# The last phase of a streaming encoder layer: row stores and x loads on GpSimd's DMA queue

## The chip, the cores and the metric

The kernel runs on one core of a Trainium2 chip. The core has a matrix engine (TensorE, PE in the profile; its weight loads are PEld), VectorE (DVE), ScalarE (ACT), GpSimd (POOL) and SyncE (SP). Each engine executes its own instruction stream in order; an instruction that waits for a semaphore holds everything behind it on that engine. DMA transfers are started by an instruction on one of these streams and carried out by 16 DMA engines that all streams share. The metric is the device time of one execution in microseconds, the median of several runs.

## What is computed

One layer of a chunk-causal encoder with two token mixers, for 2048 rows of a new stream and for 8 running streams of 16 rows that have 512 rows of cached keys and values each. Cut to what matters for the last phase:

```python
def merge_branches(oa, ob, za, zb, ga, gb, subln_g, lam_init, w_branch_a, w_branch_b, w_out):
    oa = rms_norm(oa, subln_g) * (1.0 - lam_init)
    ya = (oa.reshape(b, s, WIDTH_A) * jax.nn.silu(za)) @ w_branch_a
    yb = (ob.reshape(b, s, WIDTH_B) * jax.nn.silu(zb)) @ w_branch_b
    return (jax.nn.sigmoid(ga) * ya + jax.nn.sigmoid(gb) * yb) @ w_out
...
xp = xp + gate * merge_branches(...)
...
y_prompt = rms_norm(xp, final_g)
y_sample = rms_norm(xs, final_g)
```

`oa` and `ob` are the outputs of a differential attention and of a stick-breaking attention, both computed earlier. D_MODEL is 1024, both branch widths are 512. The sample rows need their attention over the cache too, and that work has been left for the last phase, where it runs between the matmuls.

## The kernel before

The rows are cut into 17 tiles of 128: 16 of the prompt and one (number 16, `NT`) that holds all sample rows. Earlier phases project the inputs and compute the attention of the prompt rows; they leave attention outputs in `o_d`, the gate inputs z in `z_d` and the merge gates in `g_d`, all in HBM. The last phase, from L1460 on, is a software pipeline over the tiles in the order 0 to 14, 16, 15 (`tiles`, L1379). One pass of its loop (L1593) is called a slot here. Slot n contains, for different tiles at once:

- `inputs(tiles[n + 2])` (L1311): loads of o and z into the single buffers `hs[0:2]` (L1318, L1319) and of the gates (L1325); o times z on GpSimd (L1330); scaling on VectorE (L1338), sums of squares on ScalarE (L298), a power-of-two scale on VectorE (L243 and on), and a split into two half-precision parts (L318 on ScalarE, L323 on VectorE).
- `turned(tiles[n + 1])` (L1369): transposition of these halves on TensorE (L1308, copied out on ScalarE in L1309), or from `MOVED` = 12 on by a DMA transpose (L1373).
- `branches(tiles[n])` (L1492): four groups of 12 matmuls (L1501), whose results VectorE and ScalarE gate, add and split again (L1503 to L1508).
- `turned_y(tiles[n])` (L1513): transposition of the result, on TensorE or by a DMA transpose into yT (L1517).
- `output(tiles[n - 1])` (L1523): for each half of the columns 24 matmuls (L1535), a multiplication on VectorE (L1539, into m), and the addition of x on GpSimd (L1544), in place in the tile x. In the first half it allocates x and loads its rows (L1527, L1528). The last tile adds on VectorE (L1546).
- `normed_rows(tiles[n - 2])` (L1552): the sum of squares of the finished row on ScalarE (L298).
- `stored_rows(tiles[n - 2])` (L1558): a reciprocal root on VectorE (L277 to L290), normalisation in place (L1567) and the store of 512 KB (L1568). The last tile does this in two halves (L1563, L1564).

The tile x has two buffers (tag "x"), so the load of a tile's x needs the buffer that the tile two places earlier was stored from. Before the loop the same two buffers stage the weights `wo` (L1478, split in L320 on GpSimd, L318 and L323).

Between these pieces runs the sample lane (`aside`, L1582, pieces from `sample`, L809): DMA transposes of cached keys (dks, L834), cache loads (dc, L838), loads of queries (dsam, L821), scores (L860), softmax or stick-breaking on VectorE, ScalarE and GpSimd (L688 is the stick-breaking product on GpSimd), the split of the weights (L616 on ScalarE, L619 on VectorE), their DMA transpose into dwt (L626), the products with the values (v16c; L883) and the store of o into `o_d` (L759).

Every DMA of the phase is issued from SP: `load` is `nc.sync.dma_start` (L128). SP does nothing else.

What orders the work within a slot is a list written out by hand. The matmul groups of `branches` and `output` have the places 0, 1, 2 and so on; every other piece has a place (`at`), is put behind the group numbered `at` - 0.5, and the whole is interleaved with the lane. The program order that results is then scheduled by the framework, which simulates the engines and may place an instruction earlier on its engine's stream when what it needs is there; instructions marked `keep_in_program_order` stay.

```python
        for n in range(NT + 3):
            work = branches(states[tiles[n]]) if n <= NT else []
            work += output(tiles[n - 1], states.pop(tiles[n - 1]), boxes[n - 1]) if 0 < n <= NT + 1 else []
```

Of the kernel before, what the change touches and what calls it, by code (L numbers as in the profile page):

```python
# [17 lines left out]
F32 = mybir.dt.float32  # L18
# [8 lines left out]
P = 128  # L27
D = 1024
# [30 lines left out]
H_AT = 2  # L59
Q_BUFS = 6  # L60
TR_AFTER = 5
LATE, CUTS_AT = 5, 2
LATE_ORDER = (NT - 3, NT - 1, NT - 2, NT - 5, NT - 4)
LATE_SHARE = (0, 20, 20, 20)
# [54 lines left out]
def interleave(*streams):  # L119
    for _, _, fn in interleaved(*streams):  # L120
        fn()
# [3 lines left out]
def layer_kernel(ctx: ExitStack, tc: tile.TileContext, a: dict):  # L125
    nc = tc.nc
    V, S, G, T = nc.vector, nc.scalar, nc.gpsimd, nc.tensor
    load = nc.sync.dma_start  # L128
# [45 lines left out]
    def x_rows(t):  # L174
        return x_p[t * P : (t + 1) * P, :] if t < NT else x_s

    def y_rows(t):
        return y_p[t * P : (t + 1) * P, :] if t < NT else y_s
# [32 lines left out]
    def bank(tag, dt=F32):  # L211
        return ps.tile([P, 512 if dt == F32 else 1024], dt, tag=tag, name=f"ps_{tag}", bufs=BANKS[tag])
# [343 lines left out]
    def transpose_qk(U, t):  # L556
        g, i = t // 4, t % 4
        q16, k16 = U.pop(("q16", t)), U.pop(("k16", t))
        pt = bank("t", F16)
        for c in range(2):  # L560
            T.transpose(pt[:, c * P : (c + 1) * P], k16[:, c, :, :].rearrange("p f d -> p (f d)"), id16)
        for f in range(2):
            for c in range(2):
                j = 2 + f * 2 + c
                T.transpose(pt[:, j * P : (j + 1) * P], q16[:, f, c, :, :].rearrange("p r d -> p (r d)"), id16)
        if t == NT:
            sam = stg.tile([P, 6, P], F16, tag="sam", name="sam", bufs=1)
            qst, kst = sam[:, 0:4, :], sam[:, 4:6, :]
        else:
            if i == 0:  # L570
                U["k"][g] = kvp.tile([P, 2, 512], F16, tag="k", name="k", bufs=K_BUFS)
            U["q", t] = qst = stg.tile([P, 4, P], F16, tag="qst", name="qst", bufs=Q_BUFS)
            kst = U["k"][g][:, :, i * P : (i + 1) * P]
        copy = V.tensor_copy if U["kind"] == 1 else S.copy
        copy(out=kst, in_=pt[:, 0:256].rearrange("p (c n) -> p c n", c=2))
        copy(out=qst, in_=pt[:, 256:768].rearrange("p (j n) -> p j n", j=4))  # L576
        if t == NT:
            load(out=s_d[U["u"]][:, 0:6, :], in_=sam)
# [439 lines left out]
    for m in range(len(steps)):  # L1018
        starts.append(len(line))
        for i, fn in enumerate(projection(m)):  # L1020
            line.append((m, fn))
            if i == TR_AFTER and m > 0:
                line.append((m - 1, lambda m=m: transpose_qk(units[steps[m - 1][0]], steps[m - 1][1])))
# [280 lines left out]
    def transposed(x16, dst, half):  # L1304

        pt = bank("s", F16)
        for k in range(KT):
            T.transpose(pt[:, k * P : (k + 1) * P], x16[:, half, k * P : (k + 1) * P], id16)  # L1308
        S.copy(out=dst[:, half * KT : (half + 1) * KT, :], in_=pt.rearrange("p (k n) -> p k n", n=P))  # L1309
# [69 lines left out]
    tiles = list(range(NT - 1)) + [NT, NT - 1]  # L1379
# [37 lines left out]
    for n in range(len(steps) + 2):  # L1417
        made, qk, side = [], [], []
        if n < len(steps):
            u, t = steps[n]  # L1420
# [39 lines left out]
    with ExitStack() as c2:  # L1460
        def pool2(name, bufs):
            return c2.enter_context(tc.tile_pool(name=name, bufs=bufs, reuse_waits="tile"))
# [3 lines left out]
        s2 = pool2("s2", 2)  # L1466
# [16 lines left out]
        def gate_rows(i, n):  # L1483

            pg = bank("t")
            gsm = s2.tile([P, 512], F32, tag="sg", name="gsm", bufs=2)
            load(out=gsm[0:9, :], in_=gate_d[:, n * 512 : (n + 1) * 512])
            m = 9 if i else 1
            T.matmul(pg, sel[0:9, :] if i else ones[0:1, :], gsm[0:m, :], start=True, stop=True)
            return pg  # L1490
# [22 lines left out]
        def turned_y(st, moved):  # L1513
            if moved:
                yT = dec.tile([P, NB, P], F32, tag="dc", name="yT", bufs=4).rearrange("p b n -> p (b n)")
                st["y"] = yT = yT.bitcast(F16).rearrange("p (k n) -> p k n", n=P)
                nc.sync.dma_start_transpose(out=yT, in_=L["y16"].bitcast(F16))  # L1517
                return
            st["y"] = yT = L["y"].bitcast(F16).rearrange("p (k n) -> p k n", n=P)
            for half in range(2):  # L1520
                transposed(L["y16"].bitcast(F16).rearrange("p (f n) -> p f n", f=2), yT, half)

        def output(t, st, box):  # L1523

            def half(j):
                if j == 0:
                    box["x"] = s2.tile([P, D], F32, tag="x", name="x2", bufs=2)  # L1527
                    load(out=box["x"], in_=x_rows(t))  # L1528
                x = box["x"]
                c = slice(j * 512, (j + 1) * 512)  # L1530
                po = bank("o")
                n = 0
                for yi, wi in ((0, 0), (0, 1), (1, 0)):
                    for k in range(KT):
                        T.matmul(po, st["y"][:, yi * 8 + k, :], wo[j * 4 + k // 2][:, wi, k % 2, :], start=(n == 0), stop=(n == 3 * KT - 1))  # L1535
                        n += 1
                m = s2.tile([P, 512], F32, tag="sg", name="m", bufs=2)
                if t < NT:
                    V.scalar_tensor_tensor(out=m, in0=po, scalar=st["f"][:, 1:2], in1=gate[:, c], op0=ALU.mult, op1=ALU.mult)  # L1539
                else:  # L1540
                    S.activation(out=m, in_=po, func=AF.Identity, scale=st["f"][:, 1:2])
                    V.tensor_tensor(out=m, in0=m, in1=gate_rows(1, j), op=ALU.mult)
                if t != tiles[-1]:
                    G.tensor_tensor(out=x[:, c], in0=m, in1=x[:, c], op=ALU.add)  # L1544
                    return
                V.tensor_tensor(out=x[:, c], in0=m, in1=x[:, c], op=ALU.add)  # L1546
                if j == 0:
                    box["acc"] = tiny.tile([P, 4], F32, tag="mx", name="facc")
                sum_squares(x[:, c], 512, box["acc"][:, j : j + 1])
            return [(5.2, lambda j=j: half(j)) for j in range(2)]  # L1550

        def normed_rows(t, box):  # L1552
            if t == tiles[-1]:
                return
            box["acc"] = acc = tiny.tile([P, 1], F32, tag="facc", name="facc")
            sum_squares(box["x"], D, acc, keep=True)

        def stored_rows(t, box):  # L1558
            x = box["x"]
            if t == tiles[-1]:  # L1560
                r = rsqrt_one(add_up(box["acc"], 2), D, tiny, "rF")
                for c in (slice(0, 512), slice(512, D)):
                    V.scalar_tensor_tensor(out=x[:, c], in0=x[:, c], scalar=r, in1=fg[:, c], op0=ALU.mult, op1=ALU.mult)  # L1563
                    load(out=y_rows(t)[:, c], in_=x[:, c])  # L1564
                return
            r = rsqrt_one(box["acc"], D, tiny, "rF", keep=True)
            V.scalar_tensor_tensor(out=x, in0=x, scalar=r, in1=fg, op0=ALU.mult, op1=ALU.mult)  # L1567
            load(out=y_rows(t), in_=x)  # L1568

        qpad = res.tile([P, 4, NB, 32], F16, name="qpad")  # L1570
        G.memset(qpad, 0.0)
# [20 lines left out]
        boxes = [{} for _ in tiles]  # L1592
# [3 lines that stand above are left out]
            side = []  # L1596
            if n + 2 <= NT:
                states[tiles[n + 2]], stages = inputs(tiles[n + 2])
                side += [(IN_AT[i], stage) for i, stage in enumerate(stages)]
            if n + 1 <= NT:  # L1600
                side += [(2, lambda n=n: turned(states[tiles[n + 1]], n + 1 >= MOVED)), (4.5, lambda n=n: opened(states[tiles[n + 1]]))]
            if n > 1:
                side += [(1, lambda n=n: normed_rows(tiles[n - 2], boxes[n - 2])), (2.5, lambda n=n: stored_rows(tiles[n - 2], boxes[n - 2]))]
            if n <= NT:
                side.append((4.4 if MOVED <= n < NT else 7, lambda n=n: turned_y(states[tiles[n]], MOVED <= n < NT)))
            order = [(i, 0, cost, fn) for i, (cost, fn) in enumerate(work)] + [(at - 0.5, i + 1, 0.9 if at == 7 or at == 2 and n + 1 < MOVED else 0.1, fn) for i, (at, fn) in enumerate(side)]
            work = [(cost, fn) for _, _, cost, fn in sorted(order, key=lambda e: e[:2])]
            interleave(work, aside(n) if n else [])
# [27 lines left out]
```

## Time and profile before

| | us |
|---|---|
| median of 3 runs | 2226.48 |
| lowest and highest run | 2221.84, 2226.58 |
| the profiled execution | 2225.32 |
| its span in the profile | 2223.5 |
| first and last start of the output matmuls L1535 | 1797.4, 2212.7 |

| engine | busy us in the span | share |
|---|---|---|
| TensorE | 2061.2 | 93% |
| VectorE | 1743.8 | 78% |
| ScalarE | 1606.2 | 72% |
| GpSimd | 699.6 | 31% |

The profile is one execution recorded by the hardware. A row of a timeline has the start in us from the span's start, the duration in us, the engine, the line of the kernel, the operation, the tile written and the tiles read, the shapes, a count where neighbours are merged, and in brackets how long the engine stood idle before and what ended that. "SPq" is SyncE's queue: the duration there is that of the issue, not of the transfer. A row of the waits reads: engine and line that waited, what released it, us in total, number of times, the longest. A window's row has its bounds, its length, the busy time of each engine with the number of instructions, the granted TensorE clock as a share, the mean busy share of the DMA engines and GB/s. In the chain of waits a row has the start, the duration, and the work or transfer that the end depended on.

### The profile page before, as it was taken

To read this page: it belongs to the slowest core of one execution; us is meant where nothing else is said; L and a number is where in the kernel's file an instruction comes from. 1 tells how busy PE (TensorE), PEld (TensorE's weight loads), DVE (VectorE), ACT (ScalarE), POOL (GpSimd) and SP (SyncE) were. 2 spreads that over 40 slices of the span, in tenths; PEclk is the share of its full clock that TensorE was granted. 3 is DMA by queue.
4 is the path that set the end of the run, shared out by engine and by line. 5 is a ranking of instruction groups with operands and counts; after the bars stand their busy time and mean duration, and the time that the engine had idled before them with its cause. 6 is when DMAs were issued, how large, how long until landed. Compare 5 with 4: busy or idle time off the path is not lost. (4 is left out here: it accounts for less than half of the span.)

```text
span 2223.5 us, 41495 instructions
## 1 busy us (share of the span) xinstructions
PE 2061.2 (93%) x14608; PEld 1110.4 (50%) x14608; DVE 1743.8 (78%) x3799; ACT 1606.2 (72%) x3212; POOL 699.6 (31%) x608
## 2 busy tenths in 40 slices
PE   5999999999999999999999998989998788899997
PEld 3655555555555455555554554555454444444443
DVE  4667869789887788988778888777789877787864
ACT  3978677789877677978677788876688666666531
POOL 1232014356410443742024355301334412111210
PEclk8999999999999999999999999999999899999999
DMA  9778559899796889979879999985787999999762
GB/s 323 258 241 201 120 139 217 181 227 203 200 252 158 222 201 202 207 205 221 198 195 216 191 224 207 241 181 130 159 170 155 201 280 255 230 254 224 194 166 67
DMA packets 824978, 451.05 MB, mean 203 GB/s; under 512 B 556122, under 2 KB 763274, under 8 KB 824256
## 3 DMA queue, kind: packets, MB, share of 16 engines
q1 hardware_dynamic: 823820, 448.01, 82.7%
q8 instruction: 114, 1.87, 0.3%
q14 instruction: 96, 0.79, 0.1%
q10 hardware_dynamic: 948, 0.39, 0.1%
HBM read 229.87 MB, written 86.02 MB: 142 GB/s over the span
## 5 line engine op out<-in xcount | busy, mean ns | idle before, releaser
L688 POOL TENSOR_TENSOR sc_p<-sc_p,sc_n 128x127 f32<-128x127 f32 (+7 forms) x192 | 313.3, 1635 | 663.1 <-DVE sc_n L682 510.6
L467 PEld LDWEIGHTS <-hs 128*128 128x128 f16 x3120 | 293.3, 99 | 318.5 <-issue 6.4
L467 PE MATMUL ps_mm<-wa,hs 128*128 128x512 f16 x1590 | 391.2, 382 | 5.3 <-DMA hs<-hT_d 5.0
L467 PE MATMUL ps_mm<-wb,hs 128*128 128x512 f16 x1530 | 377.4, 380 | 0.0
L682 DVE TENSOR_TENSOR_SCAN sc_n<-ps_s,sc_n,zero_t 128x512 f32<-128x512 f32 x192 | 245.4, 1278 | 33.3 <-ACT ps_s L134 28.1
L708 PE MATMUL ps_s<-k,qst 128*128 128x512 f16 (+3 forms) x640 | 223.2, 350 | 30.0 <-DVE sc_n L682 22.8
L543 PEld LDWEIGHTS <-hs 128*128 128x128 f16 x1632 | 155.0, 98 | 181.7 <-DVE qst L576 5.1
L543 PE MATMUL ps_t<-wa,hs 128*128 128x512 f16 x1020 | 242.3, 380 | 2.1 <-DVE qst L576 2.0
L619 DVE TENSOR_TENSOR sc_n<-sc_p,sc_n 128x128 f16<-128x128 f32 (+7 forms) x192 | 217.7, 1137 | 32.9 <-ACT sc_n L616 32.3
L134 ACT ACTIVATE sc_p<-ps_s,usc 128x512 f32<-128x512 f32 (+3 forms) x320 | 203.9, 637 | 34.4 <-PE ps_s L709 23.0
L709 PE MATMUL ps_s<-k,qst 128*128 128x512 f16 (+3 forms) x640 | 223.6, 350 | 0.0
L616 ACT CAST sc_n<-sc_p 128x128 f16<-128x128 f32 (+7 forms) x192 | 155.0, 809 | 57.3 <-POOL sc_p L688 55.8
L134 ACT ACTIVATE ps_s<-ps_s,usc 128x512 f32<-128x512 f32 (+3 forms) x320 | 196.3, 613 | 0.0
L543 PE MATMUL ps_t<-wb,hs 128*128 128x512 f16 x612 | 151.7, 383 | 4.8 <-DMA hs<-hT_d 2.1
L769 PE MATMUL ps_o<-v,wt 128*128 128x128 f16 x1088 | 135.2, 224 | 22.1 <-DMA wt<-sc_n 21.9
L1535 PE MATMUL ps_o<-wo,wb 128*128 128x512 f16 x624 | 141.6, 382 | 1.1 <-ACT wb L1309 1.1
L602 DVE TENSOR_SCALAR_CACHE_REDUCE sc_p<-ps_s,usc 128x512 f32<-128x512 f32 (+3 forms) x160 | 106.2, 664 | 35.7 <-PE ps_s L709 20.5
L770 PE MATMUL ps_o<-v,wt 128*128 128x64 f16 x1088 | 127.1, 196 | 0.0
L769 PEld LDWEIGHTS <-wt 128*128 128x128 f16 x1088 | 101.0, 100 | 50.1 <-DMA wt<-sc_n 25.3
L682 DVE TENSOR_TENSOR_SCAN sc_n<-ps_s,zero_t 128x128 f32<-128x128 f32 (+3 forms) x128 | 104.0, 813 | 27.7 <-ACT ps_s L134 27.7
L1501 PEld LDWEIGHTS <-wa 128*128 128x128 f16 x816 | 77.7, 98 | 94.2 <-issue 4.1
L1544 POOL TENSOR_TENSOR x<-m,x 128x512 f32<-128x512 f32 x32 | 45.6, 1427 | 247.1 <-DVE m L1539 138.7
(378 smaller groups left out, 4548.6 us busy)
## 6 DMA issues: line engine op xcount, KB each, us to landing
hs<-hT_d SPq DMA_DIRECT2D x132, 512.0 KB
g_d<-gt SPq DMA_DIRECT2D x68, 256.0 KB
out_dram<-pr SPq DMA_DIRECT2D x204, 64.0 KB
o_d<-o SPq DMA_DIRECT2D x136, 64.0 KB
wa<-g_d SPq DMA_DIRECT2D x17, 512.0 KB
wb<-g_d SPq DMA_DIRECT2D x17, 512.0 KB
hs<-o_d SPq DMA_DIRECT2D x17, 512.0 KB
wide<-in_w_ada_dram SPq DMA_DIRECT2D x8, 1024.0 KB
```

The source lines that it names most:

```text
L134: i = S.activation(**kw)
L467: T.matmul(box["p"], box["h"][:, hi, k, :], U["w"][k][:, wi, :], start=(n == 0), stop=(n == 3 * KT - 1))
L543: x = T.matmul(box["g"][:, 0:gw], box["h"][:, hi, k, :], U["wg"][k // per][:, k % per, wi, :], start=(j == 0), stop=(j == 3 * KT - 1))
L616: x = S.copy(out=hi, in_=src)
L619: V.tensor_tensor(out=lo, in0=src, in1=hi, op=ALU.subtract)
L682: V.tensor_tensor_scan(out=dst[:, lo : lo + n][:, ::-1], data0=src[:, 0:n][:, ::-1], data1=zero_t[:, 0:1].to_broadcast([P, n]), initial=fi ...
L688: G.tensor_tensor(out=p[:, 0:m], in0=p[:, 0:m], in1=n[:, 1 : m + 1], op=ALU.mult)
L708: T.matmul(p[:, 0:n], qst[:, c, :], kk[:, c, 0:n], start=True, stop=False)
L709: T.matmul(p[:, 0:n], qst[:, 2 + c, :], kk[:, c, 0:n], start=False, stop=not diag)
L769: T.matmul(po[:, c * P : (c + 1) * P], wt[:, wj, :], vt[:, c, :, :], start=first, stop=False)
L770: T.matmul(po[:, c * P : c * P + 64], wt[:, nb + wj, :], vt[:, c, 0, :], start=False, stop=last)
L1535: T.matmul(po, st["y"][:, yi * 8 + k, :], wo[j * 4 + k // 2][:, wi, k % 2, :], start=(n == 0), stop=(n == 3 * KT - 1))
```

## The change

The x tile of a row tile is allocated and loaded by a piece of its own, `rows_in`, in slot n for `tiles[n]`, one slot ahead of the output that adds to it. Its place `X_AT` is 2.8, behind that of `stored_rows(tiles[n - 2])` (2.5), which empties the same buffer. This load, and the store of finished rows of all tiles but the last, are issued from GpSimd's stream (`G.dma_start`) in place of SP's. The last tile's two half stores stay on SP.

```diff
@@ -59,6 +59,7 @@
+X_AT = 2.8
@@ -1523,9 +1524,6 @@
         def output(t, st, box):
 
             def half(j):
-                if j == 0:
-                    box["x"] = s2.tile([P, D], F32, tag="x", name="x2", bufs=2)
-                    load(out=box["x"], in_=x_rows(t))
                 x = box["x"]
@@ -1549,6 +1547,10 @@
+        def rows_in(t, box):
+            box["x"] = s2.tile([P, D], F32, tag="x", name="x2", bufs=2)
+            G.dma_start(out=box["x"], in_=x_rows(t))
+
         def normed_rows(t, box):
@@ -1565,7 +1567,7 @@
             r = rsqrt_one(box["acc"], D, tiny, "rF", keep=True)
             V.scalar_tensor_tensor(out=x, in0=x, scalar=r, in1=fg, op0=ALU.mult, op1=ALU.mult)
-            load(out=y_rows(t), in_=x)
+            G.dma_start(out=y_rows(t), in_=x)
@@ -1602,6 +1604,7 @@
             if n <= NT:
+                side.append((X_AT, lambda n=n: rows_in(tiles[n], boxes[n])))
                 side.append((4.4 if MOVED <= n < NT else 7, lambda n=n: turned_y(states[tiles[n]], MOVED <= n < NT)))
```

## The prediction

> **What bounds the kernel now.** The change touches only the last phase (the loop over 17 row tiles, from the first output matmul of L1535 at 1797 us to the end), so I read first that phase in four windows, then who kept TensorE waiting in it, then who kept SP's queue waiting, since that is the queue that loses work.
>
> ```profile
> span 2223.5 us, 41495 instructions
> core 0: us, PE busy (x) PEld busy (x) DVE busy (x) ACT busy (x) POOL busy (x), PEclk, DMA share, GB/s
> 1797.00:1880.00 83.00, 74.27 (x584) 35.95 (x583) 63.41 (x144) 55.82 (x76) 16.80 (x12) 0.98 1.03 267
> 1880.00:2080.00 200.00, 191.38 (x1487) 94.05 (x1486) 160.46 (x371) 127.53 (x176) 35.77 (x26) 1.00 0.93 236
> 2080.00:2200.00 120.00, 117.05 (x671) 53.33 (x669) 77.59 (x182) 40.41 (x61) 21.50 (x15) 1.00 0.54 147
> sum 426.50, PE 395.08 PEld 188.67 DVE 310.87 ACT 228.65 POOL 76.59; mean PE 98.77 PEld 47.17 DVE 77.72 ACT 57.16 POOL 19.15
> ```
>
> Matmuls set this phase. TensorE is idle for 8.7 us (83.00 less 74.27), 8.6 us and 3.0 us in the three windows, 20.3 us together: no edit to queues can win more than that before 2200 us. The granted clock is at or near full, so there is nothing to regain there. The DMA engines are full until 2080 us (1.03 and 0.93), POOL is busy for 76.6 of 426.5 us.
>
> The waits of TensorE from 1797 to 2200 us, and its longest wait on transposes counted from 1880 us on (last row):
>
> ```profile
> PE ps_t L883 <- DMA dwt<-dsc: 11.3, 7, 3.1
> PE ps_s L860 <- ACT wa L1309: 2.9, 1, 2.9
> PE ps_t L883 <- DVE v16c L323: 1.7, 2, 1.2
> PE ps_o L1535 <- DMA yT<-wb: 1.5, 1, 1.5
> PE ps_o L1535 <- ACT wb L1309: 0.4, 1, 0.4
> PE ps_t L883 <- DMA dwt<-dsc: 8.9, 6, 3.1
> ```
>
> More than half of the idle time ends with a DMA transpose: 11.3 us for the weights of the sample lane (dwt) and 1.5 us for yT. Both are issued from SP, so it matters what stands in front of them there:
>
> ```profile
> SPq L1568 <- DVE x L1567: 56.1, 7, 16.0
> SPq L1528 <- DMA out_dram<-x: 33.6, 12, 6.4
> ```
>
> These are the two instructions that the change takes away from SP. The store L1568 waits there for the finished rows (56.1 us), the x load L1528 for the store whose buffer it takes (33.6 us in 12 waits, 2.8 us each in the mean, 6.4 at most). For some 90 of 426.5 us SP stands still for them.
>
> **The change, part by part.** *Removed from SP:* 16 stores, 17 loads and their waits. *Moved to POOL's queue:* the same 33 DMAs with the same waits. *Moved ahead:* the x load of a tile from its own output slot to the slot before.
>
> That last part is in fact there already. Here is SP's order of one slot beside VectorE, POOL, TensorE and the chain of waits:
>
> ```profile
> 1923.95 0.34 SPq L1568 DMA_DIRECT2D out_dram<-x  x1
> 1930.75 0.33 SPq L1528 DMA_DIRECT2D x<-in_x_prompt_dram  x1
> 1931.18 0.38 SPq L1318 DMA_DIRECT2D hs<-o_d  x1
> 1928.31 1.28 DVE L323 SCALAR_TENSOR_TENSOR hs<-hs,suy,hs 128x1024 f16<-128x1024 f32 x1 [0.84 <-ACT hs L318]
> 1924.93 1.27 POOL L1544 TENSOR_TENSOR x<-m,x 128x512 f32<-128x512 f32 x1 [13.18 <-DVE m L1539]
> 1930.34 1.27 POOL L1544 TENSOR_TENSOR x<-m,x 128x512 f32<-128x512 f32 x1 [4.14 <-DVE m L1539]
> 1936.27 1.27 POOL L1330 TENSOR_TENSOR hs<-hs,hs 128x512 f32<-128x512 f32 x1 [1.86 <-issue]
> 1937.50 1.32 POOL L688 TENSOR_TENSOR dsc<-dsc 128x639 f32<-128x639 f32 x1
> 1944.92 0.24 PE L883 MATMUL ps_t<-v16c,dwt 128*32 128x128 f16 x4 [2.52 <-DMA dwt<-dsc]
> 1946.54 0.80 PE L883 MATMUL ps_t<-v16c,dwt 128*32 128x128 f16 x44 [0.63 <-DMA dwt<-dsc]
> 1923.95 6.74 DMA out_dram<-x
> 1942.67 3.83 DMA dwt<-dsc
> ```
>
> The x load is SP's next issue behind the store, as early as its buffer allows. So data arrives no earlier; what changes is who stands still.
>
> *(a) The slot above.* SP stands from the store at 1923.95 to 1930.75, and behind that wait is the load hs<-o_d, issued at 1931.18 although its buffer came free when L323 ended at 1929.6. It could go 1.6 us earlier; L1330 and, behind it on POOL, L688, whose result becomes dwt, follow, and TensorE's 2.52 and 0.63 us shrink by up to 1.6. Against it: POOL now stands there. No DMA issue of POOL is in the trace, so its length is bounded by SP's issue of the same transfer below (0.33 us, the row above) and by POOL's own 128-partition pass above (1.27 us); I take 1.27, the row of the same engine. The hold is then 1.27 for the store, the landing, 1.27 for the load: with the mean landing 5.3 us, with the longest 8.9 us. With 8.9 us from 1923.95, POOL is free at 1932.9 and then owes two adds (L1544), L688 (1.32 us), L1330 and the second L688, which starts at 1938.0 in place of 1937.50: 0.5 us late. So this slot is worth between 1.6 won and 0.5 lost; I take 0.5 won.
>
> A sentence from the pages, outside the sum: in the Trainium skill, DMA: Bandwidth & Descriptors, section Specifications, a first byte through GpSimd takes about 1 us and one through Sync or Scalar 0.6; no run here shows it, and by it, as an estimate, the hold with the mean landing would be 4.8 us in place of 5.3.
>
> *(b) yT.* The one wait on yT has this on SP and VectorE:
>
> ```profile
> 2133.30 0.35 SPq L1568 DMA_DIRECT2D out_dram<-x  x1
> 2136.00 0.33 SPq L1528 DMA_DIRECT2D x<-in_x_prompt_dram  x1
> 2136.43 1.12 SPq L1325 DMA_DIRECT2D wb<-g_d  x1
> 2137.60 4.41 SPq L1517 DMA_TRANSPOSE yT<-wb  x1
> 2135.35 0.69 DVE L1508 TENSOR_TENSOR wb<-wb,wb 128x512 f16<-128x512 f32 x1 [0.68 <-ACT wb L1507]
> 2136.78 1.27 POOL L1544 TENSOR_TENSOR x<-m,x 128x512 f32<-128x512 f32 x1 [6.11 <-DVE usq L1352]
> ```
>
> The transpose's source is ready at 2136.0 and it is issued at 2137.60, behind the x load and one gate load that came late through the store's wait. Without the two it can go 1.5 us earlier, which is all that TensorE waited. Between 1.5 won and nothing (if the x load, now on another queue, shares the engines with the transpose): 1.5 won, since the engines are half idle there (0.54).
>
> *(c) The other waits on dwt.* 11.3 less the 3.15 of (a) leaves 8.1 us. Their transposes wait for VectorE's halves and share full DMA engines; I see no x transfer as the last thing in front of them. Between 8.1 won (if SP running ahead clears them all) and nothing: nothing.
>
> *(d) The first x load.* It leaves the place behind the gate and cache loads and goes when its staging buffer is free:
>
> ```profile
> L323 DVE SCALAR_TENSOR_TENSOR wo<-x,s_w,wo x8: 1270/1283/1285, 1771.3 to 1803.9; 128x1024 f16<-128x1024 f32 x8
> 1798.53 8.72 SPq L838 DMA_DIRECT2D dc<-in_cache_a_v_dram  x3
> 1808.98 0.85 SPq L1528 DMA_DIRECT2D x<-in_x_prompt_dram  x2
> ```
>
> So at 1805 in place of 1809, beside the cache loads on which TensorE's wait of 2.9 us (L860 on L1309) hangs. 512 KB at the window's 267 GB/s are 2.0 us: between nothing and 2.0 lost, 0.8 taken, since part of the cache loads has landed by then.
>
> *(e) VectorE beside POOL's issues.* A tiny instruction that stands beside a POOL pass can take seven times as long:
>
> ```profile
> L243 DVE TENSOR_SCALAR sc_q<-usq x15: 155/170/1269, 1801.7 to 2155.9; 128x2 f32<-128x2 f32 x15
> 2136.80 1.27 DVE L243 TENSOR_SCALAR sc_q<-usq 128x2 f32<-128x2 f32 x1
> ```
>
> It starts with the POOL pass of 2136.78 and ends with it: 1.1 us above its median. If each of 33 issues did this once, VectorE would be 36 us later in sum. How much of that reaches TensorE I estimate from ScalarE, which waited 16.0 us for POOL's adds while TensorE waited 3.3 us for ScalarE (2.9 and 0.4 above), one fifth:
>
> ```profile
> ACT junk L298 <- POOL x L1544: 16.0, 9, 8.0
> ```
>
> 36 us by a fifth is 7 lost at most; nothing lost if an issue does not stand in VectorE's way. The median of 170 ns says that most tiny instructions miss POOL even now, so 0.5.
>
> *(f) The end.*
>
> ```profile
> 2218.30 0.34 SPq L1568 DMA_DIRECT2D out_dram<-x  x1
> 2219.76 0.99 SPq L1564 DMA_DIRECT2D out_dram<-x  x2
> ```
>
> The last but one tile's store goes to POOL, the last tile's two stay. Issued at 2218.30 with a landing of 2.8 us and up to 1.27 us of issue it is down by 2222.4, covered by the last stores, whose end is the span's 2223.5. With the longest landing (6.4 us, and 1.27) it ends 2.5 us late. Nothing taken.
>
> The sum: 0.5 and 1.5 won, 0.8 and 0.5 lost, 0.7 won. The profiled execution took 2225.32 us (its span and 1.8 us around it), which is 1.2 below the median of the runs, 2226.48. **Forecast: 2224.6 us.** Best ends together: 1.6, 1.5 and 8.1, so 2214; worst: 0.5, 2.0, 7 and 2.5, so 2237.
>
> **The rivals.** *SP was the limiter:* the 90 us of standing queue are the cause of the dwt waits too, SP runs a slot ahead, and (a) to (c) come in full: 2214. For it: the chain of waits goes through out_dram<-x for 6.74 us. Against it: the DMA engines are full there, so earlier issues mostly queue longer.
>
> *POOL is held (the other side):* the hold moves from SP to POOL, in front of L1544 and with it of ScalarE's sum of squares L298, which already waits for it. From store to the end of the second add there are 7.7 us in the first slot above (1923.95 to 1931.61) and 4.8 in the second (2133.30 to 2138.05), 6.2 in the mean. Hold and two adds make 7.8 us with the mean landing and 11.4 with the longest, so 1.6 to 5.2 us late in each of 15 slots, 24 to 78 in sum, a fifth of it 5 to 16: with the middle, 10 us, 2235. It decides from the point at which the hold outlasts the distance to the second add. Against it: POOL is idle four fifths of the phase.
>
> *VectorE and POOL shut each other out:* (e) in full, 2232. For it the L243 row, against it its median. The Trainium skill bears on it: SBUF — State Buffer, section Who interferes with whom, has VectorE and GpSimd share one pair of ports, with an exclusive lock in some of VectorE's modes, and says that a DMA issued from GpSimd then stalls for its descriptors. The trace agrees as far as L243 goes; that a DMA issue is hit too, no run here shows.
>
> *Nothing moves:* the load already stood behind its store, and all that goes is SP's issue time, 33 times 0.34 us, under matmuls: 2225.3. The Trainium skill has this as a rule (DMA: Bandwidth & Descriptors, Issuing engines are not separate DMA queues): all issuers share the same 16 engines, and another issuer saves only the sequencer's time. It leaves out the standing of an in-order queue, which the SP rows show.
>
> **How the numbers follow.** Two runs of this kernel can differ by 0.2%, so "same" is 2222.0 to 2230.9 around the median. The forecast has 0.32 (0.08 of it under 2222.0), SP as limiter 0.24 (0.23 faster), POOL held 0.23 (0.21 slower), shut out 0.13 (0.11 slower), nothing moves 0.08. Faster 0.31, same 0.37, slower 0.32. The forecast's own range is 2221 to 2228; to leave out no more than 2 in 10 it has to reach both sides, 2214 to 2236.
>
> **What would show it.** SP's two waits gone and hs<-o_d issued right at its buffer's release; (b) the wait on yT gone; (c) the dwt waits unchanged near 8 us; POOL waiting for out_dram<-x some 30 us in all, with ScalarE's wait for L1544 not far above 16.0; L243's maximum the same and its median not above 0.2 us; the phase's idle TensorE near 19 us. The forecast is wrong if POOL's issue takes far over 1.27 us, if ScalarE's wait for L1544 doubles, or if the dwt waits go with SP's.

## The result, and the profile after

The changed kernel takes 2231.53 us (median of 22 runs, 2222.35 to 2239.17) where the kernel before takes 2226.19 on the same chip (22 runs): ratio 1.0029, 95% interval 1.0018 to 1.004. Run a second time it is 1.0024 (1.0011 to 1.0036). So the change costs 5 to 6 us. The forecast of 2224.6 us was 1.9 us under the median on record, of which 0.7 us were the forecast gain and 1.2 us came from starting at a profiled execution below the median. The range holds the time; the direction is wrong.

In the changed kernel most lines stand one to three higher: output matmul L1533, o times z L1331, products with the values L884, score copies L1310, dwt's and yT's transposes L627 and L1518, wa's L1374, normalisation L1569; the x load is L1552 and the store L1570. In kernels with the edit by bounds shown further down the output matmul is L1536, the normalisation L1572, the store L1573, the x load L1555 on POOL and L1529 on SP.

First TensorE in the same windows as before, then its waits from 1797 to 2200 us (engine, tile and line that waited, what released it, us in all, times, longest).

```profile
1797.00:1880.00 83.00, 70.84 (x545) 35.24 (x544) 59.98 (x126) 53.00 (x72) 20.16 (x18) 0.94 0.98 259
1880.00:2080.00 200.00, 195.38 (x1519) 95.72 (x1518) 164.23 (x388) 129.87 (x180) 44.46 (x40) 1.00 0.96 236
2080.00:2200.00 120.00, 112.99 (x644) 51.50 (x643) 76.92 (x177) 40.17 (x60) 27.46 (x26) 0.97 0.57 138
```

```profile
PE ps_t L884 <- DMA dwt<-dsc: 8.2, 5, 2.8
PE ps_s L861 <- ACT wa L1310: 6.3, 1, 6.3
PE ps_o L1533 <- DMA yT<-wb: 6.1, 1, 6.1
```

TensorE's idle time is 12.2, 4.6 and 7.0 us where it was 8.7, 8.6 and 3.0. The dwt waits fell from 11.3 to 8.2 us; the one wait at the start grew from 2.9 to 6.3, the one for yT from 1.5 to 6.1. The granted clock fell to 0.94 and 0.97 in the outer windows.

**The start.** The chain of waits and the timeline of the changed kernel, then the chain and the timeline of before:

```profile
1800.34 11.98 DMA dc<-in_cache_a_v_dram
```

```profile
1800.30 0.73 POOL L1552 DMA_DIRECT2D x<-in_x_prompt_dram  x1 [1.97 <-DVE wb L1507]
1803.63 0.53 POOL L1552 DMA_DIRECT2D x<-in_x_prompt_dram  x1 [2.60 <-DVE fuy L1357]
1814.44 1.90 PE L861 MATMUL ps_s<-dks,qpad 128*32 128x512 f16 x16 [6.34 <-ACT wa L1310]
1800.00:1820.00 20.00, 13.66 (x95) 0.83 1.05 319
```

```profile
1801.55 9.16 DMA dc<-in_cache_a_v_dram
```

```profile
1812.83 1.05 PE L860 MATMUL ps_s<-dks,qpad 128*32 128x512 f16 x16 [2.85 <-ACT wa L1309]
1800.00:1820.00 20.00, 17.14 (x126) 1.00 1.03 319
```

Two x loads now go out at the moment of a cache load on which TensorE hangs. The DMA engines move the same 319 GB/s, so the cache load lands in 11.98 us in place of 9.16, TensorE waits 3.5 us longer, and the 16 matmuls behind the wait take 1.90 us in place of 1.05: the granted clock over these 20 us is 0.83 in place of 1.00.

**The transposes.** yT in the chain, the timeline and a window of the changed kernel, and the window around the same transfer before:

```profile
2135.25 12.37 DMA yT<-wb
```

```profile
2132.46 0.60 POOL L1570 DMA_DIRECT2D out_dram<-x  x1 [3.19 <-DVE x L1569]
2135.84 0.53 POOL L1552 DMA_DIRECT2D x<-in_x_prompt_dram  x1 [2.77 <-DMA out_dram<-x]
2147.66 4.02 PE L1533 MATMUL ps_o<-wo,yT 128*128 128x512 f16 x11 [6.13 <-DMA yT<-wb]
2134.00:2149.00 15.00, 8.56 (x37) 3.52 (x36) 7.86 (x16) 4.46 (x8) 2.03 (x3) 0.83 1.05 183
```

```profile
2144.08 2.55 PE L1535 MATMUL ps_o<-wo,yT 128*128 128x512 f16 x11 [1.49 <-DMA yT<-wb]
2136.00:2151.00 15.00, 13.51 (x62) 5.89 (x61) 10.65 (x30) 6.57 (x10) 2.54 (x2) 1.00 0.86 210
```

Counted from the first output matmul (1795.6 and 1797.4 us), the transpose is issued 0.55 us earlier, but the x load goes out 0.6 us behind it on the other queue, in place of 1.6 us ahead of it on the same one. It lands in 12.37 us in place of 6.43. TensorE waits 4.6 us longer for it, and the 11 matmuls behind the wait take 4.02 us in place of 2.55, at a granted clock of 0.83 over the window. In this window the DMA engines are busier (1.05 to 0.86) and move less (183 to 210 GB/s); in the other traces of this kernel and its parts that does not come again (last section).

**The end.** Here is the timeline of the changed kernel, whose span ends at 2229.8, and the store's landing (its last number) in the list of its DMA issues; in the kernel before, the rows of the prediction's (f) end at 2223.5.

```profile
2222.01 1.28 DVE L1569 SCALAR_TENSOR_TENSOR x<-x,rF,gt 128x1024 f32<-128x1024 f32 x1
2223.87 0.58 POOL L1570 DMA_DIRECT2D out_dram<-x  x1 [8.42 <-DVE r L290]
2224.81 1.02 SPq L1566 DMA_DIRECT2D out_dram<-x  x2
```

```profile
out_dram<-x POOLq DMA_DIRECT2D x1, 512.0 KB, 3.0
```

The store starts 0.58 us behind the end of the normalisation (2222.01 and 1.28), and from the start of the last half stores to the end there are 4.99 us in place of 3.74. The store from POOL is not what ends last: it is down 3.0 us behind its start, at 2226.9. SP's half stores move behind it: their packets in the trace end at 2227.84, 3.03 us behind the first half's issue, in the kernel before 2.36 us (2222.12).

**What POOL, ScalarE, VectorE and SP do.** From the waits of POOL, ScalarE and SP, and the rows of L244 (before: L243):

```profile
POOL out_dram L1570 <- DVE hs L1339: 62.3, 7, 10.6
POOL out_dram L1570 <- DVE x L1569: 46.1, 5, 13.9
POOL x L1552 <- DMA out_dram<-x: 40.9, 15, 5.0
ACT junk L299 <- POOL x L1542: 16.3, 8, 8.0
SPq L1326 <- DVE wb L1509: 32.5, 9, 9.0
SPq L1319 <- DVE hs L324: 24.9, 7, 6.0
L244 DVE TENSOR_SCALAR sc_q<-usq x17: 159/169/1320, 1757.4 to 2158.0; 128x2 f32<-128x2 f32 x17
```

POOL now stands for the finished rows and for the landing, 40.9 us in 15 waits. It does not reach ScalarE: 16.3 us, before 16.0. Tiny VectorE instructions have the same median (169 ns over these 17; the prediction's 170 is over 15 of them). SP's two waits are gone and others have come, for VectorE and for buffers.

**How the phase is measured below.** The 816 output matmuls come in 34 half groups of 24; with their starts every trace can be cut into the same pieces of work: half groups 0 to 7 (start), 7 to 24 (middle), 24 to 28 (late; these are slots 13 and 14, the first two of the four whose yT is made by DMA), 28 to the last output matmul (50.5 us in every trace), and from there to the end of the span. A stretch is one execution's; the first output matmul itself starts anywhere from 1791.1 to 1801.1 us in the 18 traces.

| us, one trace each | start | middle | late | end | sum with 50.5 |
|---|---|---|---|---|---|
| before | 96.5 | 224.8 | 43.5 | 10.8 | 426.1 |
| after | 102.0 | 219.5 | 50.1 | 12.0 | 434.2 |

### The profile page after: what moved, and what is told of

Its sections match the earlier page's. It is cut to its first block, busy times and chain, and to the rows that moved or that the text cites. A ratio compares the mean times of both kernels' runs of the same rounds, so it can differ in the third digit from the quotient of the medians.

```text
span 2229.8 us, 41488 instructions
## 1 busy us (share of the span) xinstructions
PE 2063.7 (93%) x14608; PEld 1110.9 (50%) x14608; DVE 1746.6 (78%) x3799; ACT 1604.2 (72%) x3212; POOL 719.4 (32%) x641
## 5 line engine op out<-in xcount | busy, mean ns | idle before, releaser
L709 PE MATMUL ps_s<-k,qst 128*128 128x512 f16 (+3 forms) x640 | 223.2, 350 | 29.2 <-DVE sc_n L683 22.9
L1533 PE MATMUL ps_o<-wo,wb 128*128 128x512 f16 x624 | 140.2, 379 | 0.7 <-ACT wb L1310 0.7
L509 POOL TENSOR_TENSOR rot<-pr,rope 128x256 f32<-128x256 f32 x68 | 58.5, 861 | 208.2 <-ACT pr L482 122.6
```

The source lines that it names most:

```text
L709: T.matmul(p[:, 0:n], qst[:, c, :], kk[:, c, 0:n], start=True, stop=False)
```

## The experiments

Three theories. *Sharing:* on a queue of its own a transfer no longer stands in line behind or ahead of the urgent ones, it runs beside them and stretches them. *Hold:* POOL stands between store and load and is late with its other work. *Order:* the new order of the instructions costs, whichever queue issues.

The first four below shared a chip and its runs of the kernel before, and so did each later group that is shown together. In most kernels this is the edit, with other bounds, on the changed kernel (slot n stores tile n - 2 and loads x of tile n; outside the bounds SP does it, from the old piece of the program):

```diff
             def half(j):
+                if "x" not in box:
+                    box["x"] = s2.tile([P, D], F32, tag="x", name="x2", bufs=2)
+                    load(out=box["x"], in_=x_rows(t))
...
-            G.dma_start(out=y_rows(t), in_=x)
+            queue.dma_start(out=y_rows(t), in_=x)
...
-stored_rows(tiles[n - 2], boxes[n - 2]))]
+stored_rows(tiles[n - 2], boxes[n - 2], G if 2 <= n < 99 else nc.sync))]
...
-                side.append((X_AT, lambda n=n: rows_in(tiles[n], boxes[n])))
+                if 2 <= n < 99:
+                    side.append((X_AT, lambda n=n: rows_in(tiles[n], boxes[n])))
```

This edit does more than it says where a lower bound lies inside the phase. The piece `rows_in` stands ahead of the output in a slot, so the first tile inside the bounds takes its buffer ahead of the tile before it, whose load on SP then waits for a store. SP's order and POOL's waits in first_on_sp (bounds 2 to 99):

```profile
1807.32 0.38 SPq L1529 DMA_DIRECT2D x<-in_x_prompt_dram  x1
1839.58 0.58 SPq L1529 DMA_DIRECT2D x<-in_x_prompt_dram  x1
POOL x L1545 <- DMA x<-in_x_prompt_dram: 22.4, 2, 12.3
```

The second tile's load goes at 1839.58, where the kernel before issues it beside the first (1808.98, x2). The same holds for one tile each in middle_only, only_last, loads_late, mid5 and mid5_loads_late. In only_last TensorE shows no longer waits around it (1.1 us from 2080 to 2125 us), and loads_late has it too at a ratio of 0.9997, so it need not cost; but the stretches of these kernels are not the change's parts alone.

**again**: the changed kernel once more.

> The changed kernel once more, beside the others. Three theories for its 6 us. Sharing: x's loads and stores now run beside SP's transfers in place of in line with them, and stretch the cache loads at the start of the phase (landing 12.0 us in place of 9.2) and the transpose into yT (12.4 us in place of 6.4). Hold: POOL standing for the store's landing makes its adds late. Order: the piece one slot ahead makes the scheduler lay out the phase in another order. All three: ratio 1.002 to 1.004, a TensorE wait of about 6 us on L1310 near 1814 us and one of about 6 us on yT near 2147 us. If these two waits are chance of one execution, one of them is missing here.

Measured: 1.0024 (1.0011 to 1.0036). Its trace has the start's wait (5.2 us) and three waits for yT (3.7 us in all) again; the 12.37 us of yT are not typical, here one of 8.39 us ends a wait. This execution, at 2223.51 us, was faster than the kernel's median (2227.49), and its whole phase is 426.5 us beside 426.1 and 423.4 us in two traces of the kernel before.

**stores_only**: the kernel before, with one line changed.

```diff
-            load(out=y_rows(t), in_=x)
+            G.dma_start(out=y_rows(t), in_=x)
```

> Only the 16 stores go to POOL; the x loads stay on SP at their old place. Sharing: the first x loads are in line with the cache loads again, so the wait on L1309 near 1813 us is back at about 3 us, the wait on yT is below 3 us; ratio 0.999 to 1.001. Hold: POOL stands only for the finished rows, no longer for the landing, ratio about 1.001. Order: nothing is allocated ahead, ratio 1.000.

Measured: 1.0027 (1.0016 to 1.0039), above what each of the three theories gave. Late 45.8 us, end 11.4, but the whole phase is 426.6 us, 0.5 and 3.2 us longer than in the two traces of the kernel before.

**loads_only**: the changed kernel with `load(out=y_rows(t), in_=x)`, so that only the loads are on POOL.

> Only the 17 x loads go to POOL, one slot ahead; the stores stay on SP. Sharing: both stretched transfers stay, ratio 1.002 to 1.004. Hold: POOL still stands until the store has landed, in 15 slots, ratio 1.002 to 1.004 and ScalarE's wait for POOL's adds above 16 us. Order: ratio 1.003. It tells which of the two moves carries the loss, beside stores_only.

Measured: 1.0025 (1.0012 to 1.0037). TensorE's wait at the start is 6.4 us, none is for yT (late 41.6 us); the trace's phase, 424.2 us, lies between the two of the kernel before. ScalarE waits 19.6 us for POOL's adds, as the hold theory had it; so this kernel does not tell sharing from hold.

**ahead_on_sp**: the order of the changed kernel, with both on `load`.

> The x load one slot ahead as in the change, but load and store on SP as before. Sharing and hold: nothing left of the loss, ratio 0.999 to 1.001, SP's waits for the store's landing near 34 us as before. Order: the loss stays, ratio 1.002 to 1.004.

Measured: 0.9997 (0.9987 to 1.0008). This order costs nothing that can be measured.

**first_on_sp**, **last_on_sp**, **middle_only**: bounds 2 to 99, 0 to 12 and 2 to 12.

> The change, but the loads of the first two x tiles stay on SP at their old place, behind the cache loads; all else on POOL. Sharing: the last cache load lands in about 9 us again and the TensorE wait on L1310 near 1814 us falls from 6 to about 3 us, the wait on yT stays near 6 us; ratio lower than the full change's by 0.001 to 0.002. Hold and order: 15 slots still stand, ratio 1.002 to 1.004.

> The change up to slot 11; from slot 12, where the transposes of y go by DMA, stores and x loads are on SP as before. Sharing: the wait on yT falls from 6 to below 2 us, the wait near 1814 us stays at 6; ratio lower than the full change's by 0.001 to 0.002. Hold: 10 of 15 slots still stand, ratio about 1.002.

> Both at once: POOL's queue only for slots 2 to 11. Sharing: both long waits of TensorE are gone and what the freed SP queue wins in the middle is left (8.6 against 4.6 us of idle TensorE between 1880 and 2080 us), so ratio 0.997 to 1.000, below both kernels. Hold: 10 of 15 slots stand, ratio about 1.002.

Measured: 1.0009 (0.9995 to 1.0023), 1.0000 (0.9987 to 1.0014) and 1.0006 (0.9993 to 1.002). The last two keep ten of the 15 holds, and POOL waits 26.9 and 29.2 us for landings in them: the hold in those slots costs nothing that can be measured. Without the late slots nothing measurable is lost. But first_on_sp, which has the late slots and the end of the change, has nothing within its interval too. In its chain the cache load lands as before:

```profile
1799.75 9.21 DMA dc<-in_cache_a_v_dram
```

**only_first**, **only_last**, **tail_only**, **stores_early**: bounds 0 to 2, 12 to 99, 17 to 99; and the kernel before with the stores of slots 2 to 11 on POOL.

> Only the first two x loads go through POOL's queue, at the place of the change; every store and every other x load is on SP at the old place. Sharing theory (the transfers of POOL's queue stretch the urgent ones of SP's queue at the start and at the end of the phase): the cache load in front of the first score copies lands in about 12 us in place of 9.2, TensorE's wait there is 5.5 to 6.5 us in place of about 3, the 16 matmuls behind it take 1.9 in place of 1.05, and the ratio to the kernel before is about 1.0018 (4 us). Hold theory (POOL's stream stands between store and load and makes its adds late): no store and no wait for a landing is on POOL, so the ratio is 1.000.

> Only from slot 12 on do stores and x loads go through POOL's queue; the slots before are as in the kernel before. Sharing theory: at the start the landing is 9.2 us and TensorE's wait about 3; at the end a yT lands in 8 to 12 us in place of 6.4, TensorE's waits for yT are 3 to 6 us, the last half stores take 4.4 to 5.0 us to the end of the span in place of 3.7, together 2 to 5 us: ratio 1.001 to 1.002. Hold theory: 5 of 15 holds are left, a third of the loss of the whole change: about 1.0008.

> Only one store, that of the last but one tile, goes through POOL's queue. Sharing theory: from the start of the last half stores to the end of the span 4.4 to 5.0 us in place of 3.7, from the last output matmul to the end of the span 11.4 to 12.0 in place of 10.8; the ratio is 1.0003 to 1.0005, at the limit of what can be measured. Hold theory: 1.000 and 3.7 us. If the loss of stores alone (1.0027) sat in this one store, the ratio would be near 1.002.

> The stores of slots 2 to 11 go through POOL's queue, the later stores and all x loads through SP's at the old place. It is the first part of the kernel with stores alone on POOL (ratio 1.0027). Sharing theory: nothing urgent stands beside these stores, so the ratio is 1.000 and the end is as before (yT landing about 6.4 us, 3.7 us from the last half stores to the end). If the loss of that kernel comes from SP's x loads, which then wait in front of the lane's loads for a landing of another queue (62 us in ten waits there), 10 of 15 such waits are left and the ratio is about 1.0017.

Measured: 1.0004 (0.9989 to 1.0019), **1.0021 (1.0005 to 1.0038)**, 1.0008 (0.9992 to 1.0023) and 1.0004 (0.9989 to 1.002). The late slots alone bring most of the change's loss as measured, with an interval of 1 to 8 us. The start's mechanism is clean, the chain and the timeline of only_first have it whole. Of the 3 to 4 us that it loses by the end of the start the ratio shows 0.9 (0.0004 of 2222 us), with an interval that holds both nothing and 4 us; last_on_sp, which has the start's wait too (5.6 us), measures 1.0000:

```profile
1799.07 12.04 DMA dc<-in_cache_a_v_dram
```

```profile
1813.24 1.90 PE L861 MATMUL ps_s<-dks,qpad 128*32 128x512 f16 x16 [5.96 <-ACT wa L1310]
```

In the chain of only_last, yT is stretched, with the x load 0.18 us behind its issue in the timeline:

```profile
2158.12 8.41 DMA yT<-wb
```

```profile
2158.30 0.54 POOL L1555 DMA_DIRECT2D x<-in_x_prompt_dram  x1 [2.65 <-DMA out_dram<-x]
```

**stores_late**, **loads_late**, **before_again**: only one of the two in the late slots (stores with 12 <= n < 17 on the kernel before, loads with n >= 12 on loads_only), and the kernel before once more.

> Stores of slots 12 to 16 on POOL (not the last but one tile's), all else on SP at the old place. Late-slots theory, by the kernels run so far: from the first output matmul on, the time between the output matmuls at 321.3 us (2118.8 in the profile of before) and 364.7 us (2162.2) is 43.4 us with late stores on SP (41.7 to 43.6 in seven kernels) and 45.5 to 50.1 us with late stores on POOL; so 45 to 46 us here, yT waits of TensorE of 2 to 3 us, the end from the last half stores 3.7 us as before, ratio about 1.001. If it is the x load on POOL beside the transpose and not the store that costs, 43.4 us, yT 1.5 us, ratio 1.000.

> x loads of slots 12 to 16 on POOL at the place of the change, all stores and the earlier x loads on SP. Late-slots theory: as in the kernel with all loads on POOL, where these 43.4 us were 41.7 and TensorE never waited for yT, nothing is lost: ratio 1.000, yT at most 1.5 us. If an x load on a queue of its own beside the transpose stretches it, yT lands in 8 us or more, TensorE waits 3 us for it and the ratio is about 1.0015.

> The kernel before once more, as a measure of how far a ratio and the stretches of a single trace lie from each other without any change: ratio 1.000 with an interval of some 0.0015 to each side, the stretch of 43.4 us within 0.5, TensorE's wait for yT 1.5 us and its first longer wait on the score copies 2.9 us. A ratio beyond 1.002 would say that the small ratios of the other kernels are no evidence.

Measured: 1.0005 (0.9994 to 1.0017), 0.9997 (0.9983 to 1.001) and 1.0004 (0.9993 to 1.0015). The last row says what a ratio is worth: below some 1.0015 nothing is shown by one. The late stretch of the traces separates better: 45.7, 41.4 and 43.2 us: in the traces it is the store on POOL that costs in the late slots, 2.5 us alone; its ratio is too small to show it. The timeline of loads_late has an x load 0.13 us ahead of yT's transpose, and TensorE does not wait for yT at all (the last row has no wait in brackets):

```profile
2130.45 0.59 POOL L1555 DMA_DIRECT2D x<-in_x_prompt_dram  x1 [5.85 <-DVE wb L1509]
2130.58 5.38 SPq L1518 DMA_TRANSPOSE yT<-wb  x1
2139.74 10.52 PE L1536 MATMUL ps_o<-wo,yT 128*128 128x512 f16 x48
```

So an x load beside it is not enough to make TensorE wait for yT. A small stretch would not show there, since TensorE comes for yT 9.2 us behind its issue; by the packets of the trace the transpose's last one ends 6.9 us behind the issue, in the kernel before 6.0. In only_last and after the x load goes out behind the transpose and not ahead of it; what that does was not tested. In stores_late the second yT lands in 6.45 us, no longer than before, but is issued later: 13.5 us behind the first yT matmul ahead of it (2159.52 less 2146.01), where before_again has 11.3 (2148.67 less 2137.39). Chain and timeline of stores_late, then timeline of before_again:

```profile
2159.52 6.45 DMA yT<-wb
```

```profile
2144.07 0.51 SPq L1528 DMA_DIRECT2D x<-in_x_prompt_dram  x1
2144.69 0.37 SPq L1318 DMA_DIRECT2D hs<-o_d  x1
2146.01 2.55 PE L1535 MATMUL ps_o<-wo,yT 128*128 128x512 f16 x11 [0.95 <-DMA yT<-wb]
2149.75 1.26 POOL L1330 TENSOR_TENSOR hs<-hs,hs 128x512 f32<-128x512 f32 x1 [9.23 <-DMA hs<-o_d]
2151.05 0.88 DVE L1338 SCALAR_TENSOR_TENSOR hs<-hs,orms,hs 128x128 f32<-128x128 f32 x3 [2.75 <-POOL hs L1330]
2157.17 0.69 DVE L1508 TENSOR_TENSOR wb<-wb,wb 128x512 f16<-128x512 f32 x1
2158.49 0.35 SPq L1528 DMA_DIRECT2D x<-in_x_prompt_dram  x1
```

```profile
2135.37 0.56 SPq L1318 DMA_DIRECT2D hs<-o_d  x1
2137.39 2.55 PE L1535 MATMUL ps_o<-wo,yT 128*128 128x512 f16 x11 [1.57 <-DMA yT<-wb]
2139.66 1.27 POOL L1330 TENSOR_TENSOR hs<-hs,hs 128x512 f32<-128x512 f32 x1 [8.53 <-DMA hs<-o_d]
2140.96 0.88 DVE L1338 SCALAR_TENSOR_TENSOR hs<-hs,orms,hs 128x128 f32<-128x128 f32 x3 [1.47 <-POOL hs L1330]
2147.27 0.69 DVE L1508 TENSOR_TENSOR wb<-wb,wb 128x512 f16<-128x512 f32 x1
2147.65 0.34 SPq L1528 DMA_DIRECT2D x<-in_x_prompt_dram  x1
2148.67 4.67 SPq L1517 DMA_TRANSPOSE yT<-wb  x1
```

The order of SP explains part of it. In the kernel before the x load stands ahead of yT's transpose (2136.00 and 2137.60 in (b)); with the store gone from SP the framework has placed it behind, right ahead of the load hs<-o_d. That load is issued 0.7 us later against the matmul and takes 5.1 us to its reader L1330 in place of 4.3, so that VectorE starts L1338 1.5 us later, and behind L1338 on VectorE stands the rest of the slot up to yT's halves (L1508), which are ready 1.3 us later. The other 0.9 of the 2.2 us pass on SP between the halves and the transpose, where the x load, which waits for the landing of POOL's store until 2158.49, and a gate load stand ahead of it. Which of these ended last was not settled.

**mid5**, **mid5_loads_late**: a search for a version that keeps the middle's gain: bounds 5 to 12; and the loads from 5 to 17.

> Stores and x loads of slots 5 to 11 on POOL at the places of the change, all others on SP at the old places. By the output matmuls the phase falls into four stretches, which without the change last 92.1 to 92.9 (start), 225.9 to 229.0 (middle), 43.2 to 43.5 (late) and 61.3 us (end, to the end of the span), and with it 94.1 to 97.9, 223.7 to 223.8, 46.1 to 50.1 and 62.5. If these parts stand by themselves, this kernel has 92.5, 224, 43.4 and 61.3, some 4 us less than before: ratio about 0.998. If the gain in the middle is only the start's loss regained (a lane that was held up early runs up behind), the middle is 227 to 229 here and the ratio 1.000.

> As the kernel with slots 5 to 11 on POOL, and the x loads of slots 12 to 16 on POOL too, whose stores stay on SP. If the parts stand by themselves: 92.5, 224, 41.5 and 61.1 us, some 6 us less than before, ratio about 0.9975. If the middle's gain is only the start's loss regained: 1.000 or, by the late loads alone (0.9997 by themselves), 0.999.

Measured: 1.0000 (0.9989 to 1.001) and 0.9992 (0.998 to 1.0004). The middle is 222.1 and 221.0 us by the table's bounds (the expectations end the start 4.1 to 4.2 us earlier, at a row within half group 6): the first is within the kernel before's 221.9 to 224.8, the second between that and the 219.5 of the changed kernel. The ratios are those that were forecast for a gain that only regains the start's loss, not 0.998 and 0.9975. No version beats the kernel before by more than can be measured.

The traces together, grouped by what runs on POOL:

| us | kernels | range |
|---|---|---|
| start, nothing on POOL in it | before, before_again, tail_only, only_last, stores_late, loads_late, ahead_on_sp, mid5, mid5_loads_late | 96.2 to 98.1 |
| start, first two x loads on POOL | after, again, only_first, last_on_sp, loads_only | 98.2 to 102.0 |
| start, only stores or later x loads on POOL | first_on_sp, middle_only, stores_only, stores_early | 97.7 to 100.0 |
| start and middle together, at most two DMAs on POOL, at the end | before, before_again, tail_only, only_last, stores_late, loads_late, ahead_on_sp | 318.9 to 321.8 |
| the same, all on POOL | after, again, last_on_sp | 317.9 to 321.5 |
| the same, a part on POOL | only_first (323.7), first_on_sp, middle_only, stores_only, stores_early, loads_only, mid5, mid5_loads_late | 318.4 to 323.7 |
| late, nothing on POOL | before, before_again, tail_only, only_first, middle_only, last_on_sp, ahead_on_sp, stores_early, mid5 | 41.8 to 43.6 |
| late, stores on POOL | after, again, first_on_sp, only_last, stores_only, stores_late | 45.5 to 50.1 |
| late, loads alone on POOL | loads_only, loads_late, mid5_loads_late | 41.4 to 41.6 |
| end, last but one store on SP | the twelve others | 10.6 to 11.1 |
| end, that store on POOL | after, again, first_on_sp, only_last, tail_only, stores_only | 11.4 to 12.0 |

The late stretch and the end keep their groups apart, by 1.9 and 0.3 us. The start doesn't: its groups touch.

## Why the prediction was wrong

In the traces the loss is in the late stretch and the end: by the table 2 to 6.6 us and 0.6 to 1.2 us above the 43.5 and 10.8 of before. What the start loses, the middle has back in the three kernels with both on POOL, but not in only_first, whose start and middle take 323.7 us. The sum of late and end, 3 to 8 us, holds the 5 to 6 of the ratios. The ratios bear it out in part: only_last has most of the loss and last_on_sp none, but first_on_sp, with the same late slots, measures 1.0009, stores_late 1.0005, and loads_only 1.0025 with nothing lost in these stretches. So where the loss sits is shown for single traces, and for the medians only made likely. None of the rivals was this; the lower bound of (b) named the sharing, but at nothing lost.

*(a) and (c)*: SP does issue hs<-o_d when its buffer is free (its wait L1319 for L324 says so), and the dwt waits went from 11.3 to 8.2 us, by what (a) hoped for and to the 8.1 of (c). But the second trace of the kernel before has 8.1 too, so the drop is no proof of a gain, and start and middle together show none.

*(b) is the step that failed.* It took 1.5 us won "since the engines are half idle there (0.54)". That is the mean of 120 us; in the 15 us of the transposes the share was 0.86 already. With store and load on POOL TensorE's wait for yT went from 1.5 to 6.1 us (3.7 in the second trace), and the late stretch lost 2 to 6.6 us, where (b) had nothing as its worst end. The prediction looked at two neighbours on SP and let all else stand; in the traces two other things follow. Transposes that TensorE waits for land in 8.4 to 12.4 us beside store and load on the other queue (5.4 to 6.8 in the other kernels), and in the kernels with the stores alone on POOL SP's x load, no longer held ahead of yT by the store's wait, comes in front of hs<-o_d. Which share each has in the whole change was not separated; loads_late shows that TensorE doesn't wait for yT beside an x load on POOL so long as the stores stay on SP. Why the store's queue decides it stays open.

*(d)* had the mechanism right and the size wrong: 0 to 2.0 lost by the bytes of one x load at the window's rate, 0.8 taken. There were two loads, TensorE waited 3.5 us longer and lost 0.85 us on matmuls at a lower clock. What of it reaches the end of the kernel, the ratios of only_first and last_on_sp don't show.

*(e)* nothing, as nearly taken. *(f)* took nothing where 0.6 to 1.2 us are lost: the store starts 0.55 us later than from SP, and the half stores, which it thought would cover it, move behind it and end later.

*POOL's issue* was put at 1.27 us by the row of another operation. The issue shows 0.60 us, with 0.58 us between the end of the normalisation and its start, where SP's stores started 0.03 us behind it (2133.30 in (b), with L1567's end at 2133.27). So 1.18 us pass, but POOL is recorded as busy for half of it. ScalarE's 16.3 us and last_on_sp's 1.0000 speak against *POOL is held*, and L244's median against *shut out*. *SP was the limiter* fell too: SP's two waits went, others came, and nothing was won.

The Trainium skill, DMA: Bandwidth & Descriptors, section Issuing engines are not separate DMA queues, says that transfers of all issuers interleave on the same 16 engines. The trace agrees: 319 GB/s at the start before and after, with one cache load 2.8 us longer.

**Left open.** stores_only and loads_only each measure about 1.0025, while their single traces show a phase of 426.6 and 424.2 us beside 423.4 and 426.1 for two traces of the kernel before. What they lose outside these traces was not found, and neither was why the late slots cost 2 us in one execution and 6.6 in another; 4.6 of the 6.6 are the longer wait for yT and 1.5 the slower matmuls behind it. A third x buffer, which would take the load's wait for the store away, wasn't tried.

## What to carry to other kernels

An in-order queue that stands for a wait can also keep bulk transfers out of the way of urgent ones; here the first cache load landed in 11.98 us in place of 9.16 once the x loads no longer stood behind it. Before moving transfers to a second queue, list the urgent transfers that they will then run beside, at the DMA share of those microseconds and not of the phase. Whether a recovered wait counts is read from whole stretches: cut the traces at the same pieces of work and compare stretch by stretch, with a second run of the kernel before as the measure, and put every trace into a group, also the ones that don't fit. When an edit moves a tile's allocation in some passes of a loop only, look at the order in which the buffers are then taken.

## What was unexpected of the hardware

- After a wait of TensorE of 5.2 to 6.4 us, 16 score matmuls took 1.90 us in place of 1.05 (five traces); after 2.6 to 3.2 us they did not in ten traces, but did in two, after 2.92 (loads_late, first row below) and 3.03 us (mid5_loads_late), and took 1.32 us in mid5 after 2.93. The Trainium skill, TensorE: Matmul & The Clock Gate, section What's actually happening, has the clock halved after an idle window of about 3.4 us. The second row below, a window of loads_late with the granted clock behind the busy time, agrees with the halving (0.51); the length of one wait alone does not decide it in these traces.

```profile
1810.21 1.90 PE L861 MATMUL ps_s<-dks,qpad 128*32 128x512 f16 x16 [2.92 <-ACT wa L1310]
1810.00:1813.00 3.00, 2.79 (x25) 0.51 1.02 405
```

- In the changed kernel 13 of the 16 stores from POOL begin 0.58 us behind the normalisation that they wait for (two 0.30 us), from SP it is 0.03 us where nothing else holds the store.
- In one execution only, while transposes and an x load on another queue ran together, the DMA engines were busier and moved less: 1.05 and 183 GB/s beside 0.86 and 210. It did not come again: the same stretch of 15 us has 0.93 and 234 in again, 0.92 and 237 in only_last, and 0.87 and 211 in before_again.
